# A gated block with dilated attention on one core: VectorE, ScalarE and POOL take program order, the softmaxes over head groups are weighted earlier, the pool mixer's gates come first

## Chip, cores and metric

One core of one Trainium2 chip. The metric is device time in microseconds. The change is compared with the kernel before it; a measurement of this kernel tells differences of about 0.3% from no change.

## What is computed

One decoder block on x (2048 tokens x 1024), in fp32, then a final RMSNorm. Cut to what matters:

```python
h = rmsnorm(x, norm_g) * (1 + scale) + shift             # scale, shift, gate = c @ w_ada + b_ada
qkv, z_attn, u_pool, z_pool, g_attn, g_pool = split(h @ w_in)
for gi, (win, dil) in enumerate(((128, 1), (512, 4), (2048, 16))):     # 8 heads of 64 each
    o, lse = dilated_window_attention(q, k, v, dil, win // dil, bias_g)
wts = softmax(stack(lses), axis=0)                        # over the three head groups
attn = sum(wts[..., None] * stack(outs), axis=0)
y_attn = (attn * silu(z_attn)) @ w_attn_br
pooled = multiscale_pool(u_pool)                          # trailing means over 2, 4, 8, 16 minus the token
mixed = einsum('bsgc,gce->bsge', pooled, pool_w) * pool_scale
y_pool = (mixed * silu(z_pool)) @ w_pool_br
merged = sigmoid(g_attn) * y_attn + sigmoid(g_pool) * y_pool
out = rmsnorm(x + gate * (merged @ w_out), final_g)
```

## The kernel before

The tokens are two halves `h` of 1024. Every big product is `mm3` (L247): operands are split into a high and a low fp32r part, and three products (hi hi, hi lo, lo hi) of two 128x512 matmuls each make a k-step, eight k-steps a 128x1024 tile in PSUM. Weights stream in through `fetch_raw` (a DMA on SyncE's queue) and `fetch_part`, which casts the high part on VectorE (L217) and subtracts the low part on POOL (L218).

For each half, four head pairs `hp` and three groups g in the order 1, 2, 0 make a `unit` (24 k-steps for the columns of k, q and v). `weave` runs the `attention` generator of the unit before inside it, some k-steps and then one step of attention. A step s of attention works on several pairs of 128-token tiles p at once: `transposed(s-2)` turns the exponentials (PE L717; VectorE L723, L726 and ScalarE L727 copy them to the single buffer pT), `output(s-3)` multiplies them with v (PE L738), `logits(s)` makes the next ones (PE L682, VectorE L686, ScalarE L692, VectorE L701, POOL L702), and `differences` (POOL L632) makes vd, with a single buffer, for the outputs. For g = 0 the outputs of the three groups are joined: `load_rows` fetches the other two groups' outputs and softmax terms, the weights are made by VectorE with one exp on ScalarE (L752 to L767), the three outputs are weighted and added (L770, L773), and in the next step `joined(s-4)` transposes the sum on PE (L777), after which ScalarE copies it to attnT (L779). PSUM tiles of `tp()` ("knot") have two buffers: output and joined of a step share one bank, transposed uses the other. Eight steps s = 0 to 7 make such an attention of g = 0; steps 3 to 7 are the ones in which output and joined run.

The last unit of a half (hp = 3, g = 0) is woven with `pool_in` instead of a unit: u's columns for the four groups of the pool mixer, a step each four k-steps. `pool_out` then makes the gates (zp's columns, sigmoid L820) and mixes. `branch`, `attn_gate`, `branch` and two `out_half` follow. In the second `out_half` of half 0, `next_h` prepares the normalised input of half 1: x tiles are loaded (`new_x`), squared and scaled (`x_norm`, ScalarE L293, POOL L282, VectorE L295) and transposed (`transposed_x`, PE L340, ScalarE L345).

After the first unit only PE and SyncE keep the order in which the program is written; the order on VectorE, ScalarE and POOL is chosen by a scheduler (L1051). The rotating buffers `b4` of the pool "big" are shared by nearly all of these tiles, so a load into one may wait for its last reader.

Of the kernel before, what the change touches and what calls it, by code (L numbers as in the profile page):

```python
# [11 lines left out]
F32 = mybir.dt.float32  # L12
# [56 lines left out]
def stream():  # L69
# [6 lines left out]
    seq += [("in", OFF_U + c * P, "col") for c in range(4)]  # L76
    seq += [("in", OFF_ZP + c * P, "col") for c in range(4)]
    for off, br in ((OFF_GP, "pbr"), (OFF_GA, "abr")):
# [68 lines left out]
def block_kernel(ctx: ExitStack, tc: tile.TileContext, x, cols, b_gate, w_ada, wpk, pool_w, rel_bias, final_g, onehot,  # L147
# [278 lines left out]
    def next_h(hp_, tiles):  # L426

        for p in range(0, 8, 2):
            for i, _ in enumerate(transposed_x(tiles[p:p + 2], p, hp_)):
                if p and p < 6 and i in (3, 4):  # L430
                    x_norm(tiles[p + i - 1])
                yield
            if p < 4:
                tiles += [new_x(1, p + 4), new_x(1, p + 5)]
# [150 lines left out]
    def attention(h, g, hp, res):  # L585
# [143 lines left out]
        def output(p, bank):  # L729
# [11 lines left out]
            if g:  # L741
# [16 lines left out]
            e = sm.tile([P, 2, 3, 2], F32, name="e")  # L758
# [26 lines left out]
        for s in range(7 if g else 8):  # L785
# [11 lines left out]
            for p in parts_:  # L797
                next(p, None)
# [12 lines left out]
            for p in parts_:  # L811
                next(p, None)
# [17 lines left out]
    def branch(hparts, gated, merged, mparts=None):  # L830
# [4 lines left out]
        for u in range(4):  # L835
# [3 lines left out]
            for j in range(2):  # L839
                ps = mm()  # L840
                yield from mm3(ps, take("col"), hparts)
# [7 lines left out]
                yield from mm3(ps, wb, gated, slice(j * P, (j + 1) * P), frees=(j == 1))  # L849
# [12 lines left out]
    def pool_in(h, hparts, pooled, todo):  # L862

        for gi in range(4):
            ps = mm()
            for _ in mm3(ps, take("col"), hparts):
                next(todo[0], None) if todo else None
                yield
            cur = b4(name="u0")
            nc.scalar.copy(out=cur, in_=ps)  # L870
            todo[:] = [chain(*todo, pool_sums(h, gi, cur, pooled))]

    def pool_sums(h, gi, u0, pooled):
# [25 lines left out]
        split(phi, plo, cur)  # L899
# [10 lines left out]

    def pool_out(hparts, pooled, gated, pwh, pwl, todo):
        for gi in range(4):
            ps = mm()
            for _ in mm3(ps, take("col"), hparts):
                next(todo[0], None)
                yield
            assert len(pooled) > gi
            sg = sigmoid(ps)
            nc.vector.tensor_tensor(out=sg, in0=ps, in1=sg, op=ALU.mult)
            phi, plo = pooled[gi]  # L920
            gsl = slice(gi * P, (gi + 1) * P)
            for q in range(2):
                sl = slice(q * 512, (q + 1) * 512)
                ps = bank(q)
                for i, (w, m) in enumerate(((pwh, phi), (pwh, plo), (pwl, phi))):
                    nc.tensor.matmul(ps, lhsT=w[:, gsl], rhs=m[:, sl], start=(i == 0), stop=(i == 2))  # L926
                nc.vector.scalar_tensor_tensor(out=sg[:, sl], in0=ps, scalar=psc_col[:, gi:gi + 1], in1=sg[:, sl],
                                               op0=ALU.mult, op1=ALU.mult)
            ghi, glo = b4(F32R, "gphi"), b4(F32R, "gplo")
            split(ghi, glo, sg)  # L930
# [205 lines left out]
```

## Time and profile before

| | us |
|---|---|
| median of 3 runs | 2218.45 |
| fastest, slowest run | 2213.07, 2219.28 |
| the profiled execution's own time | 2212.21 |
| its span, first to last instruction | 2210.2 |
| PE busy in it | 2137.7 (97%) |
| VectorE, ScalarE, POOL busy | 933.1, 597.6, 805.9 |
| mean granted TensorE clock | 0.989 |

All durations below come from that one profiled execution. [...] In the rows, the number in brackets behind an instruction is its engine's idle time before it, and what ended it.

### The profile page before, as it was taken

What the parts mean: (1) busy time and instruction counts of PE and PEld (TensorE: products, weight loads), DVE (VectorE), ACT (ScalarE), POOL (GpSimd) and SP (SyncE); (2) the same over time, 40 slices, a digit from 0 to 9 for tenths busy, and PEclk for the clock granted to TensorE, in tenths of its full rate; (3) what the DMA queues carried; (4) which work ended last, traced back from release to release, by engine and by line L of the source; (5) the groups of instructions that cost most, each with busy time, mean ns of one, the idle gap of its engine ahead of it and who ended that gap; (6) DMA issues with size and microseconds to landing.
All of it is one profiled execution on the core that took longest, in us unless ns stands there. A gap on an engine that the chain in (4) does not pass through costs nothing.

```text
span 2210.2 us, 30824 instructions
## 1 busy us (share of the span) xinstructions
PE 2137.7 (97%) x11786; PEld 1808.5 (82%) x11786; DVE 933.1 (42%) x2144; ACT 597.6 (27%) x1487; POOL 805.9 (36%) x669
## 2 busy tenths in 40 slices
PE   6999999999999999999799999999999999999998
PEld 4888888888878888889778878888888788888898
DVE  6536335263382111117743464553644831111164
ACT  4423333233321001003433333333333310010023
POOL 3313222132243225437743232332333432253375
PEclk9999999999999999999999999999999999999999
DMA  8442232222211112114432333223222111121134
GB/s 294 142 153 73 81 95 73 73 74 80 76 60 42 48 48 87 52 43 172 162 120 87 89 90 89 72 82 111 81 81 86 53 48 48 48 86 48 48 134 162
DMA packets 142675, 198.48 MB, mean 90 GB/s; under 512 B 13542, under 2 KB 109983, under 8 KB 142528
## 3 DMA queue, kind: packets, MB, share of 16 engines
q1 hardware_dynamic: 142528, 196.51, 27.9%
q8 instruction: 93, 1.52, 0.3%
q14 instruction: 54, 0.44, 0.1%
HBM read 157.62 MB, written 35.16 MB: 87 GB/s over the span
## 4 chain that ended last, share of the span: by engine, by line
PE 42%; DVE 3%; DMA 2%; issue 2%; POOL 2%; ACT 1%; SPq 0%; POOLq 0%; DVEq 0%; ACTq 0%
PE mm L255 33%; PE mm L1003 3%; PE knot L738 3%; PE qk L682 2%; DMA row<-rows 1%; POOL wlo L218 1%; PE knot L717 1%; PE knot L646 1%; ACT l L692 1%; DMA wraw<-in_wpk_dram 1%; DVE wd L762 0%; DVE l L701 0%; DVE whi L217 0%; PE hp L926 0%; POOL y L982 0%
## 5 line engine op out<-in xcount | busy, mean ns | idle before, releaser
L218 POOL TENSOR_TENSOR wlo<-wraw,whi 128x512 fp32r<-128x512 f32 x352 | 476.4, 1357 | 995.9 <-DVE whi L217 549.6
L255 PE MATMUL mm<-hhi,whi 128*128 128x512 f32 x2000 | 637.8, 400 | 0.0
L255 PE MATMUL mm<-hlo,whi 128*128 128x512 f32 x2000 | 621.4, 392 | 0.0
L255 PE MATMUL mm<-hhi,wlo 128*128 128x512 f32 x2000 | 619.5, 391 | 0.0
L217 DVE CAST whi<-wraw 128x512 fp32r<-128x512 f32 x349 | 189.6, 547 | 754.0 <-PE mm L255 628.7
L255 PEld LDWEIGHTS mm<-hhi,wlo 128*128 128x128 f32 x2000 | 377.4, 189 | 81.8
L255 PEld LDWEIGHTS mm<-hlo,whi 128*128 128x128 f32 x2000 | 377.1, 189 | 81.4
L255 PEld LDWEIGHTS mm<-hhi,whi 128*128 128x128 f32 x2000 | 364.7, 189 | 72.0 <-issue 0.5
L820 ACT ACTIVATE sg<-mm 128x1024 f32<-128x1024 f32 x48 | 49.4, 1028 | 555.1 <-PE mm L255 443.2
L686 DVE CUSTOM_DVE_ANT_0 l<-qk,bias 128x256 f32<-128x256 f32 (+1 forms) x384 | 126.0, 384 | 129.2 <-PE qk L682 105.9
L692 ACT ACTIVATE l<-l,row 128x256 f32<-128x256 f32 (+1 forms) x256 | 117.2, 460 | 149.0 <-DVE row L686 126.7
L1003 PE MATMUL mm<-whi,mhi 128*128 128x256 f32 x512 | 149.2, 291 | 1.0 <-DVE yt L1032 0.7
L1003 PE MATMUL mm<-whi,mlo 128*128 128x256 f32 x512 | 146.2, 286 | 2.5 <-POOL mlo L827 2.5
L1003 PE MATMUL mm<-wlo,mhi 128*128 128x256 f32 x512 | 145.9, 285 | 0.0
L738 PE MATMUL knot<-v,pT 128*128 128x64 f32 x768 | 131.5, 270 | 3.2 <-ACT pT L727 2.9
L738 PEld LDWEIGHTS knot<-v,pT 128*128 128x128 f32 x768 | 112.7, 193 | 5.7 <-ACT pT L727 3.2
L702 POOL TENSOR_TENSOR l<-l,ident 128x512 f32<-128x512 f32 (+1 forms) x56 | 71.6, 1278 | 108.5 <-DVE l L701 97.7
L738 PE MATMUL knot<-vd,pT 128*128 128x64 f32 x560 | 109.6, 278 | 1.3 <-DVE wd L762 1.3
L1003 PEld LDWEIGHTS mm<-whi,mlo 128*128 128x128 f32 x512 | 99.2, 194 | 3.3 <-POOL mlo L827 3.3
L1003 PEld LDWEIGHTS mm<-whi,mhi 128*128 128x128 f32 x512 | 99.5, 194 | 1.9 <-DVE yt L1032 1.5
L1003 PEld LDWEIGHTS mm<-wlo,mhi 128*128 128x128 f32 x512 | 99.5, 194 | 0.1
L727 ACT COPY pT<-knot 128x512 f32<-128x512 f32 x96 | 56.4, 588 | 155.1 <-PE knot L738 67.7
(175 smaller groups left out, 2497.3 us busy)
## 6 DMA issues: line engine op xcount, KB each, us to landing
wraw<-in_wpk_dram SPq DMA_DIRECT2D x176, 512.0 KB, 3.7
rows<-row SPq DMA_DIRECT2D x128, 66.0 KB, 1.7
row<-rows SPq DMA_DIRECT2D x64, 132.0 KB, 3.4
wada<-in_w_ada_dram SPq DMA_DIRECT2D x32, 256.0 KB, 5.5
x<-in_x_dram SPq DMA_DIRECT2D x16, 512.0 KB, 6.3
y<-in_x_dram SPq DMA_DIRECT2D x16, 512.0 KB, 7.7
out_dram<-yo SPq DMA_DIRECT2D x16, 512.0 KB, 6.5
khist<-kh SPq DMA_DIRECT2D x52, 128.0 KB, 2.5
```

The source lines that it names most:

```text
L217: copy(out=hi, in_=raw)
L218: nc.gpsimd.tensor_tensor(out=lo, in0=raw, in1=hi.bitcast(F32), op=ALU.subtract)
L255: nc.tensor.matmul(ps[:, n * 512:(n + 1) * 512], lhsT=w, rhs=m[:, n * 512:(n + 1) * 512], start=(k == 0 and j == 0), stop=(k == nk - 1 and ...
L646: nc.tensor.transpose(ps[:, (t % 4) * P:(t % 4) * P + P], res["vT"][:, k0:k0 + P], ident)
L682: nc.tensor.matmul(qks[i][:, j * 256:j * 256 + nk], lhsT=qt[qi][a], rhs=keys[ki][a], start=(n == 0), stop=(n == 2))
L686: nc.vector.tensor_tensor_reduce(out=l[:, 2 * j + i, 256 - nk:], in0=qks[i][:, j * 256:j * 256 + nk], in1=bt[:, i, 256 - nk:], scale=-1.0, ...
L692: nc.scalar.activation(out=ll, in_=ll, func=AF.Exp, scale=-1.0, bias=nd[:, j, i:i + 1], accum_out=nd[:, j, 2 + i:3 + i])
L702: nc.gpsimd.tensor_tensor(out=prev, in0=prev, in1=ident.unsqueeze(1).broadcast_to([P, 4 - f, P]), op=ALU.mult)
L727: nc.scalar.copy(out=pT[:, 1], in_=pps)
L738: nc.tensor.matmul(ops[:, j, hs], lhsT=d["pT"][:, b, 2 * j + i, :], rhs=vv[:, hs], start=(b == 1), stop=(b == 0 or not full))
L820: nc.scalar.activation(out=s, in_=ps, func=AF.Sigmoid)
L1003: nc.tensor.matmul(pst[:, pos:pos + 256], lhsT=st, rhs=mv, start=(fresh and i == 0), stop=(last and i == 2))
```

## The change

1. The manual schedule covers VectorE, ScalarE and POOL too, so that all five engines run in the order in which the program is written.
2. For g = 0 a new function `weights(p)` makes the weights of pair p, and weights and adds the two loaded groups, in step p + 3, between the VectorE work of `transposed` and that of `output`. The group's own output is added by four `scalar_tensor_tensor` (VectorE) that read PSUM, in place of ScalarE's copy (L751) and of the third plane of L770 and L773.
3. The pool mixer's gates (`pool_gates`: zp's columns, sigmoid) now come first, woven with the last attention of the half; u's columns follow (`pool_mix`, groups 3 down to 0), and each group's sums, mixing and split run as a generator `pool_group` that later k-steps `advance`, the last of them into the first product of `branch`.
4. `next_h` loads two x tiles at i = 3 instead of after i = 7 and runs `x_norm` at i = 4, 5 instead of 3, 4. In the output stage y is normalised in place, and yt, the gate's row and final_g's row move to buffers of the attention that are idle then, so that no x load waits for those.

```diff
+            r3, e = d["row3"], d["e"]
+            for j in range(2):
+                for i in range(2):
+                    hs = slice(i * 64, (i + 1) * 64)
+                    nc.vector.scalar_tensor_tensor(out=r3[:, j, 0, hs], in0=ops[:, j, hs], scalar=e[:, j, 2, i:i + 1],
+                                                   in1=r3[:, j, 0, hs], op0=ALU.mult, op1=ALU.add)
-            r3 = d["row3"]
-            nc.scalar.copy(out=r3[:, :, 2, 0:P], in_=ops)
-            nc.vector.tensor_copy(out=r3[:, :, 2, P:], in_=d["nd"])
-            yield
+        def weights(p):
+            d = st[p]
+            r3, nd = d["row3"], d["nd"]
+            nc.vector.tensor_copy(out=r3[:, :, 2, P:], in_=nd)
...
             for j in range(2):
-                ov = r3[:, j, :, 0:P].rearrange("p g (h c) -> p g h c", c=64)
-                nc.vector.tensor_tensor(out=ov, in0=ov, in1=e[:, j].unsqueeze(3).broadcast_to([P, 3, 2, 64]),
+                ov = r3[:, j, 0:2, 0:P].rearrange("p g (h c) -> p g h c", c=64)
+                nc.vector.tensor_tensor(out=ov, in0=ov, in1=e[:, j, 0:2].unsqueeze(3).broadcast_to([P, 2, 2, 64]),
                                         op=ALU.mult)
-            for i in (1, 2):
-                nc.vector.tensor_tensor(out=r3[:, :, 0, 0:P], in0=r3[:, :, 0, 0:P], in1=r3[:, :, i, 0:P], op=ALU.add)
+            nc.vector.tensor_tensor(out=r3[:, :, 0, 0:P], in0=r3[:, :, 0, 0:P], in1=r3[:, :, 1, 0:P], op=ALU.add)
...
-            for p in parts_:
+            for i, p in enumerate(parts_):
+                if i == len(parts_) - 1 - (s > 3) and g == 0 and 3 <= s < 7:
+                    weights(s - 3)
                 next(p, None)
...
-            for p in parts_:
-                next(p, None)
             yield
...
-                if p and p < 6 and i in (3, 4):
-                    x_norm(tiles[p + i - 1])
+                if p and p < 6 and i in (4, 5):
+                    x_norm(tiles[p + i - 2])
+                if p < 4 and i == 3:
+                    tiles += [new_x(1, p + 4), new_x(1, p + 5)]
...
-                    ctx.enter_context(tc.manual_schedule(engines={et.PE, et.SP}))
+                    ctx.enter_context(tc.manual_schedule(engines={et.PE, et.SP, et.DVE, et.Activation, et.Pool}))
...
-        weave(pool_in(h, hparts, pooled, todo), 32, queue, n_queue, 1)
-        run(queue)
-        run(pool_out(hparts, pooled, gated, pwh, pwl, todo))
-        run(branch(hparts, gated, merged))
+        weave(pool_gates(hparts, sgs), 32, queue, n_queue, 1)
+        run(queue)
+        todo = []
+        run(pool_mix(h, hparts, sgs, gated, pwh, pwl, todo))
+        run(branch(hparts, gated, merged, todo=todo))
```

How the order moves, at three places. The first is VectorE in the attention of g = 0, half 1, head pair 0, from step 3 to step 4; `row_...` is a pair's row3, numbered anew in each kernel. Before:

```order
L686 ISA nd 128x1
L773 TENSOR_TENSOR row_10665<-row_10665 128x2x128 x2
L701 TENSOR_TENSOR l<-l 128x4x128
L217 CAST whi<-wraw 128x512
L723 TENSOR_TENSOR pT<-knot,prevm 128x512
L770 TENSOR_TENSOR row_10738<-row_10738,e 128x3x128
L726 TENSOR_TENSOR pT<-pT,l 128x512
L770 TENSOR_TENSOR row_10738<-row_10738,e 128x3x128
L752 COPY row_10899<-nd 128x2x4
L563 SCALAR_TENSOR_TENSOR qlo_10844<-mm,qhi_10843 128x1024
```

And the same stretch after the change, from the end of step 3's transposed to step 4's:

```order
L726 TENSOR_TENSOR pT<-pT,l 128x512
L760 COPY row_10699<-nd 128x2x4
L763 TENSOR_REDUCE mn<-row_10699 128x4
L766 TENSOR_TENSOR e<-mn,row_10699 128x12
L769 TENSOR_TENSOR wd<-e,row_10699 128x12
L771 TENSOR_REDUCE sd<-wd 128x4
L773 RECIPROCAL sd<-sd 128x4
L774 TENSOR_TENSOR e<-e,sd 128x12
L777 TENSOR_TENSOR row_10699<-row_10699,e 128x2x128 x2
L779 TENSOR_TENSOR row_10699<-row_10699 128x2x128
L753 SCALAR_TENSOR_TENSOR row_10699<-knot,e,row_10699 128x64 x4
L686 ISA l,nd<-qk,bias 128x256
```

The whole weighting of a pair and the four reads of PSUM (L753) now stand in one piece between transposed's products and the next logits (L686), where before pieces of several pairs were mixed.

The second place is ScalarE in the same attention, steps 4 and 5 after the change (L767 is the weights' exp, L785 the copy of joined to attnT, L562 the high part of q of the unit that runs beside it):

```order
L692 ACTIVATE l,nd<-l,nd 128x256 x4
L727 COPY pT<-knot 128x512
L767 ACTIVATE e<-e 128x12
L785 COPY attnT_10532<-knot 128x256
L562 ACTIVATE qhi_10881<-mm 128x1024
L727 COPY pT<-knot 128x512
```

The copy to attnT stands ahead of q's high part, and no copy of the group's own output is left.

The third place is ScalarE in `next_h`, around the squares of the second pair of x tiles (L293) and those of the output stage (L983 before, L1008 in the change); L345 is the copy of a transposed tile. Before:

```order
L293 ACTIVATE junk,ssq<-x_8845 128x1024
L345 ACTIVATE hraw<-hp,shift_c,gmul 128x256
L983 ACTIVATE yt_9000,ssq_8598<-y_8596 128x256
L983 ACTIVATE yt_9000,ssq_8601<-y_8599 128x256
L983 ACTIVATE yt_9000,ssq_8604<-y_8602 128x256
L983 ACTIVATE yt_9000,ssq_8607<-y_8605 128x256
L293 ACTIVATE junk,ssq<-x_8847 128x1024
L345 ACTIVATE hraw<-hp,shift_c,gmul 128x256
```

After the change:

```order
L293 ACTIVATE junk,ssq<-x_8762 128x1024
L345 ACTIVATE hraw<-hp,shift_c,gmul 128x256
L293 ACTIVATE junk,ssq<-x_8764 128x1024
L345 ACTIVATE hraw<-knot,shift_c,gmul 128x256
L1008 ACTIVATE yt,ssq_8632<-y_8630 128x256
L1008 ACTIVATE yt,ssq_8635<-y_8633 128x256
```

The second tile's square now stands ahead of the output stage's four squares, not behind them.

## Rows read from the trace of the kernel before

**Rows 1.** The page's busy us, share of span, instructions, by engine

```profile
PE 2137.7 (97%) x11786; PEld 1808.5 (82%) x11786; DVE 933.1 (42%) x2144; ACT 597.6 (27%) x1487; POOL 805.9 (36%) x669
```

**Rows 2.** Stretches: length, busy us by engine, PEclk, DMA share, GB/s

```profile
200.00:240.00 40.00, 38.18 (x213) 31.69 (x212) 18.52 (x53) 11.70 (x37) 10.03 (x10) 0.96 0.31 94
600.00:640.00 40.00, 37.69 (x206) 31.56 (x204) 36.88 (x86) 12.22 (x36) 18.05 (x13) 0.91 0.15 50
640.00:680.00 40.00, 37.84 (x172) 31.12 (x172) 23.96 (x38) 9.49 (x12) 21.74 (x11) 1.00 0.18 53
1080.00:1120.00 40.00, 23.37 (x169) 22.78 (x168) 23.69 (x45) 16.70 (x42) 20.81 (x29) 0.79 0.27 93
1280.00:1320.00 40.00, 36.32 (x204) 30.36 (x203) 22.51 (x54) 12.27 (x32) 10.48 (x9) 0.96 0.27 76
1720.00:1760.00 40.00, 35.03 (x172) 29.60 (x171) 38.44 (x73) 10.51 (x25) 15.50 (x10) 0.91 0.22 63
...
1093.06:1097.06 4.00, 4.00 (x21) 4.00 (x22) 3.89 (x7) 1.02 (x2) 3.19 (x3) 0.56 0.02 6
```

**Rows 3.** PE's waits: us in total, times, longest us

```profile
PE knot L777 <- DVE row L773: 17.9, 11, 3.6
PE hp L340 <- DVE x L295: 16.6, 3, 8.0
...
PE knot L738 <- ACT pT L727: 2.9, 1, 2.9
...
PE hp L340 <- ACT hraw L345: 1.7, 1, 1.7
PE knot L738 <- DVE wd L762: 1.3, 1, 1.3
```

**Rows 4.** PE's timeline, one g = 0 unit: start us, us, instruction

```profile
1423.66 0.39 PE L738 MATMUL knot<-vd,pT 128*128 128x64 f32 x2
...
1429.54 0.33 PE L738 MATMUL knot<-v,pT 128*128 128x64 f32 x2
...
1436.09 0.33 PE L738 MATMUL knot<-v,pT 128*128 128x64 f32 x2
...
1439.84 0.44 PE L777 MATMUL knot<-ident,row 128*128 128x128 f32 x2 [1.85 <-DVE row L773]
...
1444.23 0.33 PE L738 MATMUL knot<-v,pT 128*128 128x64 f32 x2
...
1448.94 0.38 PE L777 MATMUL knot<-ident,row 128*128 128x128 f32 x2
```

**Rows 5.** VectorE's timeline in the same unit

```profile
1428.01 0.42 DVE L686 CUSTOM_DVE_ANT_0 l<-qk,bias 128x256 f32<-128x256 f32 x1
...
1430.65 0.70 DVE L701 TENSOR_TENSOR l<-l 128x512 f32<-128x512 f32 x1 [0.38 <-ACT l L692]
...
1433.17 1.78 DVE L726 TENSOR_TENSOR pT<-pT,l 128x512 f32<-128x512 f32 x1
...
1439.28 0.17 DVE L756 TENSOR_REDUCE mn<-row 128x4 f32<-128x12 f32 x1 [1.79 <-DMA row<-rows]
1439.37 0.41 DVE L773 TENSOR_TENSOR row<-row 128x256 f32<-128x256 f32 x1
...
1440.76 0.17 DVE L767 TENSOR_TENSOR e<-e,sd 128x12 f32<-128x12 f32 x1
```

**Rows 6.** POOL's timeline in the same unit

```profile
1432.79 1.60 POOL L218 TENSOR_TENSOR wlo<-wraw,whi 128x512 fp32r<-128x512 f32 x1
...
1438.13 0.72 POOL L632 TENSOR_TENSOR vd<-v 128x256 f32<-128x256 f32 x1 [2.59 <-DMA wraw<-in_wpk_dram]
```

**Rows 7.** Groups by line: busy us, mean ns, idle before

```profile
L727 ACT COPY pT<-knot 128x512 f32<-128x512 f32 x96 | 56.4, 588 | 155.1 <-PE knot L738 67.7 <-DVE pT L723 66.9 <-DVE row L752 11.3
...
L820 ACT ACT_TABLE_LOAD x2 | 2.6, 1283 | 4.0 <-PE mm L255 4.0
...
L404 DVE SCALAR_TENSOR_TENSOR gmul<-scale_c,col 128x2 f32<-128x2 f32 x4 | 0.9, 222 | 0.1
```

More of the change, by code (lines that the diff above doesn't have):

```diff
@@ L75, in stream @@
             seq += [("in", b + 512, "col"), ("in", b, "col"), ("in", b + 1024, "col")]
-    seq += [("in", OFF_U + c * P, "col") for c in range(4)]
     seq += [("in", OFF_ZP + c * P, "col") for c in range(4)]
+    seq += [("in", OFF_U + c * P, "col") for c in range(3, -1, -1)]
     for off, br in ((OFF_GP, "pbr"), (OFF_GA, "abr")):
@@ L828, in msplit, with branch @@
         return [(hi[:, j * 512:(j + 1) * 512], lo[:, j * 512:(j + 1) * 512]) for j in range(2)]
[L830 removed]
+    def branch(hparts, gated, merged, mparts=None, todo=()):
         add = bool(merged)
@@ L840, in branch @@
                 ps = mm()
-                yield from mm3(ps, take("col"), hparts)
+                for _ in mm3(ps, take("col"), hparts):
+                    advance(todo)
+                    yield
+                run(*todo)
                 sg = sigmoid(ps)
@@ L848, in branch @@
                 ps = mm()
-                yield from mm3(ps, wb, gated, slice(j * P, (j + 1) * P), frees=(j == 1))
+                turn = -1 if todo and not (u or j) else 1
+                yield from mm3(ps, wb[::turn], gated[::turn], slice(j * P, (j + 1) * P), frees=(j == 1))
                 msl = slice(j * 512, j * 512 + 512)
@@ L860, in branch, with pool_gates, pool_mix @@
             mparts += msplit(merged[0][3])
-    def pool_in(h, hparts, pooled, todo):
+    def pool_gates(hparts, sgs):
         for gi in range(4):
             ps = mm()
+            yield from mm3(ps, take("col"), hparts)
+            sg = sigmoid(ps)
+            nc.vector.tensor_tensor(out=sg, in0=ps, in1=sg, op=ALU.mult)
+            sgs.append(sg)
+    def pool_mix(h, hparts, sgs, gated, pwh, pwl, todo):
+        gated += [None] * 4
+        for gi in range(3, -1, -1):
+            ps = mm()
             for _ in mm3(ps, take("col"), hparts):
-                next(todo[0], None) if todo else None
+                advance(todo)
                 yield
@@ L870, in pool_in, with advance, pool_group @@
             nc.scalar.copy(out=cur, in_=ps)
-            todo[:] = [chain(*todo, pool_sums(h, gi, cur, pooled))]
+            todo.append(pool_group(h, gi, cur, sgs, gated, pwh, pwl))
+    def advance(gens):
+        for i in gens:
+            next(i, None)
+    def pool_group(h, gi, u0, sgs, gated, pwh, pwl):
+        pooled, n = [], 0
+        for _ in pool_sums(h, gi, u0, pooled):
+            n += 1
+            yield
+        for _ in range((7, 8, 10, 11)[gi] - n):
+            yield
+        sg = sgs[gi]
+        phi, plo = pooled[0]
+        gsl = slice(gi * P, (gi + 1) * P)
+        for q in range(2):
+            sl = slice(q * 512, (q + 1) * 512)
+            ps = bank(q)
+            for i, (w, m) in enumerate(((pwh, phi), (pwh, plo), (pwl, phi))):
+                nc.tensor.matmul(ps, lhsT=w[:, gsl], rhs=m[:, sl], start=(i == 0), stop=(i == 2))
+            nc.vector.scalar_tensor_tensor(out=sg[:, sl], in0=ps, scalar=psc_col[:, gi:gi + 1], in1=sg[:, sl],
+                                           op0=ALU.mult, op1=ALU.mult)
+        ghi, glo = b4(F32R, "gphi"), b4(F32R, "gplo")
+        split(ghi, glo, sg, nc.gpsimd if gi else nc.vector)
+        gated[gi] = ghi, glo
     def pool_sums(h, gi, u0, pooled):
@@ L909, in pool_weights @@
         return pwh, pwl
[L911 to L930, printed above, removed]
-            gated.append((ghi, glo))
     def attn_gate(h, hparts, gated):
@@ L989, in normed @@
             r = rstd(ssq, nc.gpsimd)
-            yo = b4(name="yo")
-            nc.vector.tensor_tensor(out=yo, in0=y, in1=fg_bc, op=ALU.mult)
-            nc.scalar.activation(out=yo, in_=yo, func=AF.Copy, scale=r)
+            for i in range(2):
+                sl = slice(i * 512, (i + 1) * 512)
+                nc.vector.tensor_tensor(out=y[:, sl], in0=y[:, sl], in1=fg_bc[i], op=ALU.mult)
+            nc.scalar.activation(out=y, in_=y, func=AF.Copy, scale=r)
             t0 = h * HALF + (4 * q + p) * P
-            store(out[t0:t0 + P, :], yo, 2)
+            store(out[t0:t0 + P, :], y, 2)
         for n in range(4):
@@ L1070, in block_kernel @@
         run(branch(hparts, gated, merged, m0))
-        rows_bc = b4(name="gate"), b4(name="fg")
+        rows_bc = (att.tile([P, D], F32, name="gate", tag="pT", bufs=1),
+                   [att.tile([P, 512], F32, name="fg", tag="bias", bufs=2) for _ in range(2)])
         nc.sync.dma_start(out=rows_bc[0], in_=gate_d)
-        nc.sync.dma_start(out=rows_bc[1], in_=final_g.partition_broadcast(P))
+        for i in range(2):
+            nc.sync.dma_start(out=rows_bc[1][i], in_=final_g[i * 512:(i + 1) * 512].partition_broadcast(P))
         mparts = []
```

10 lines of the change are left out of this document (4 added, 6 removed).

## The prediction

> **What bounds the kernel now.** I read the page's busy times first: PE is busy for 97% of the span [rows 1], so a change can only give back what PE spends idle or at its lower clock, and can only cost by making PE wait. Next, PE's waits by line [rows 3]: the joined transposes L777 wait 17.9 us for VectorE's last addition L773, 11 times; the transposes of half 1's input L340 wait 16.6 + 1.7 us; the last units add 2.9 and 1.3 us at L738. The start of the program waits too, and is not touched. Then the stretches [rows 2], for the clock: where PE had stood still for some us, its granted clock falls to the lower level. [...]
>
> Three places therefore have something to win. **The last unit of each half**: PE misses 2.31 + 2.16 us in the two stretches of half 0 and 4.97 us in that of half 1, 9.44 us in all; 0.91 over 40 us is 7.2 us at half rate, 3.6 us lost, twice: 16.6 us. **Six regular units of g = 0**: L777's 17.9 us less the last units' share of it (9.44 less L738's 4.2, so 5.2) leaves 12.7 us; three of the six show the 0.96 (the first and the last of these stretches are in the rows), 4.8 us: 17.4 us. **The input of half 1**: 18.3 us of waits. The clock is at 0.56 in the four us behind the longest of them, in which PE never stops; that is 3.5 us at half rate, 1.75 lost, and I count the same once more behind the last one (0.79 over 40 us has 16.8 us at the lower level, of which most lies in the waits themselves): 21.8 us.
>
> **Regular units of g = 0.** PE's order is the same; VectorE's is new. I follow one unit by PE's own times [rows 4] and VectorE's durations [rows 5].
>
> The price of one pair's weights: from L756's start to L767's end 1.65 us, the exp on ScalarE in it; with the copy ahead 1.75. Then three 256-element operations at 0.41 (two products, one addition), some 1.2 us: 2.95 us in a row. The four scalar_tensor_tensor of 64 elements don't occur before; below they are bounded by the same operation on two elements, 0.22 us [rows 7], whose start mostly overlaps, above by an L773 of four times the size, 0.41. I take 0.18 each, nearest to the first: 0.7 us. So 3.65 us, all in VectorE's order, and all ahead of the next logits.
>
> Step 3: PE ends output(0) at 1424.05; only then is the single pT free. L723 and L726 take 0.7 each, POOL's vd (0.72 [rows 6]) delays what follows by about 0.5: 1426.0. With 3.65 the weighting ends at 1429.7. PE's output(1), due at 1429.54, takes the same PSUM bank: it waits **0.25 us**.
>
> Step 4: the last logits stand behind that. From the first L686 to L701 pass 2.64 us, so L701 starts at 1432.3, L723 ends at 1433.5. POOL's L702 starts with L701's end, and an L726 beside a POOL operation takes 1.78 us instead of 0.7 [rows 5, 6]: 1434.9; vd again holds VectorE's next operations for some 0.65: 1435.55. With 3.65: 1439.2. ScalarE's copy to attnT (0.38) and a handover of 0.1: 1439.7. Output(2) is due at 1436.09 + 0.25 and takes the bank that all these read: it waits **3.35 us**.
>
> That the copy to attnT stands in this chain rests on one bank being read by two engines. In the trace ScalarE's L727 loses 66.9 us behind VectorE's L723 [rows 7], although both only read the same transposed bank. [...]
>
> Step 5: output(2) ends at 1441.45. q's high part, now behind the copy on ScalarE, and its low part on VectorE hold VectorE to 1441.85, a weight cast to 1442.25; L723 to 1442.85; L726 beside the cast's POOL operation L218 (1.3 to 1.6 us) to 1444.2, vd to 1444.9; 3.65 more: 1448.55. Joined(2) of step 6 was due at 1444.23 + 1.73 - 1.85 + 0.25 + 3.35 = 1447.7: **0.9 us**. Step 6: the next cast and its L218 (to 1450.2), then 3.65: 1453.9; joined(3) was due at 1448.94 - 1.85 + 4.5 = 1451.6: **2.3 us**.
>
> That is 6.8 us a unit. A wait of 3.35 us drops the clock as the one of 3.6 did, for 1.6 us; 0.9 of it falls where joined(2) would have waited anyway: 0.7. So 7.5 us a unit, 45.0 in six, against 17.4: **+27.6 us**. Whether POOL's operations meet VectorE's chain is the open part. If VectorE always goes first, step 4's vd and L702 (2 us) and step 6's L218 (1.3) drop out, and a unit loses some 3.8; if each meets it fully, three times another 1.1 us (1.78 less 0.69), 10.8.
>
> **Last units.** The same chain, but a step each four k-steps instead of three, as the program weaves them. Outputs are 6.55 us apart [rows 4]; some 2.5 of it are attention's own matmuls (output 1.73, the rest transposes), so a k-step is about 1.35 us, and three steps gain 4.0 us of the 7.5 and leave 3.5. The sigmoids of the gates stand between the exps, and each change of function loads a table: 12 more loads at 1.28 us [rows 7], 15.4 us of ScalarE, nearly all in its idle time; about half a load per half delays an exp, 0.6. So 4.1 in each half, 8.2 against 16.6: **-8.4 us**; nothing lost at all would be -16.6, the same waits as before no gain. The later groups' sums run under k-steps that PE has to do anyway; the last one (group 0) is needed at the end of branch's first product, where I see no more than a us of slack.
>
> [...]
>
> **Input of half 1.** The two x loads of a pair start four k-steps earlier and find free buffers; the second tile's square no longer stands behind the output stage's four squares. I take the longest wait, 8.0, as gone, the other 8.6 us of L340 as halved (4.3), the 1.7 as halved (0.8), the clock's 3.5 as 2.3, since a wait of 2 us can still drop it: 7.4 us against 21.8, **-14.4 us**. The ends are 0 and -21.8; of the three waits of x the longest is the one that the swapped rows explain whole.
>
> **The rest.** At the very end the reductions and products of the last two tiles alternate: +0.4. Units of g = 1 and 2 have no weights; program order can delay their loads of keys: +1.0 (0 to 5). The arithmetic that left (the third plane of L770, one L773, ScalarE's copy) ran beside PE: 0 in itself.
>
> **Sum**: 27.6 - 8.4 - 14.4 + 0.4 + 1.0 = **+6.2 us**. The profiled execution took 2212.2, 6.2 less than the median of the runs; on it the change gives 2218.4, on the median 2224.7.
>
> **The rivals.** (a) *POOL mostly loses the port*: a unit loses 3.8, 22.8 in six, +5.4 instead of +27.6, total -16.0: 2202.5. For it: VectorE is busy for only 42% of the span [rows 1], so most chains may find POOL idle; against: program order puts L726 right behind the L701 that starts POOL's L702. (b) *The weights are in time*, which is what moving them ahead would do if logits and pT did not hold them: each unit loses 1 us at most, -11.4 there, total -32.8: 2185.7. It decides if the weighting of pair 1 ends before PE wants output(2), at 1436.1; by the rows it ends three us later. (c) *Slower: POOL takes the port in the middle of each chain.* Three operations more stretched as L726 was, 3.2 us a unit, 19.2 in six: 2243.9. It decides if POOL's L218 and vd begin before the chain's first operation in steps 4, 5 and 6; the 1.78 us row speaks for it, the short operations of the chain, which can slip between, against. (d) *The reordering does not do what it says*: the scheduler before already kept these waits down as far as the data allow, the units stay at 17.4, and input and last units are held by other things: no change, 2218.5 to 2220.
>
> **How the numbers follow.** Forecast 0.45, with a range of its own from 2215 (units of 6) to 2236; (a) 0.22; (b) 0.10; (c) 0.17; (d) 0.06. A measurement tells 0.3%, 6.7 us: faster is below 2211.8, slower above 2225.1. Faster: (b) and most of (a), 0.27. Within: the lower half of the forecast, the rest of (a), and (d), 0.33. Slower: the forecast's upper half and (c), 0.40. The range 2194 to 2242 leaves out (b) and half of (c).
>
> **What would show it.** Right: in the six units PE waits at L738 for ScalarE's copy to attnT about 3 us at step 5 and at joined for L753 1 to 2 us at step 7, 40 us in all; L340 waits below 8 us; the windows of the last units at PE 38 or more of 40. Wrong: no L738 wait for the copy (then (b)); a wait of 5 us or more there, with L726 or the products above 1.5 us (then (c)); L340's longest wait still near 8 us.

## The result, and the profile after

The changed kernel takes 2248.18 us (median of 4 runs, 2247.62 to 2249.28), the kernel before 2217.9 beside it: a ratio of 1.0141, 95% interval 1.0123 to 1.0159. It is slower by 1.4%, some 30 us, where +6.2 was forecast and the range ended at 2242. The profiled executions have spans of 2245.8 and 2210.2 us; the account below is of these 35.6 us. The mean granted clock fell from 0.989 to 0.981.

The two programs give PE the same number of instructions, in the same order outside the pool stage, so the start of the n-th can be compared in the two traces. What the later one loses between two such marks is the difference of a stage (plus is time lost):

```
stage                                          forecast   after
start of the program                              0        -0.3
six regular units of g = 0                      +27.6     +24.5   (3.9 3.6 5.2 in half 0, 1.5 5.2 5.2 in half 1)
two last units, pool stage behind them           -8.4      -6.5
first output product of half 0, of half 1         0       +12.5, +6.3
input of half 1 (second output product)         -14.4      -1.6
units of g = 1 and 2                              +1.0       0.0
very end                                          +0.4      +0.7
```

**The units.** PE's waits by line in the changed kernel, the view of [rows 3]:

```profile
PE knot L738 <- ACT attnT L785: 22.8, 8, 3.2
PE hp L340 <- DVE x L295: 6.9, 3, 3.7
PE mm L1029 <- POOL wlo L218: 6.7, 6, 1.9
...
PE hp L340 <- ACT hraw L345: 3.6, 1, 3.6
PE mm L1029 <- DVE yt L1043: 3.6, 3, 1.7
...
PE knot L738 <- DVE row L753: 2.8, 6, 0.6
```

Joined, which waited 17.9 us before [rows 3], waits 2.3 us in all now; output waits for the copy to attnT instead, 3.15 to 3.17 us in each regular unit and 1.9 us in each of the last two. The timeline of VectorE in the unit of [rows 4, 5], 21.46 us later now:

```profile
1450.46 0.86 DVE L753 SCALAR_TENSOR_TENSOR row<-knot,e,row 128x64 f32<-128x64 f32 x4
...
1453.86 0.69 DVE L701 TENSOR_TENSOR l<-l 128x512 f32<-128x512 f32 x1 [1.17 <-ACT l L692]
1454.47 0.68 DVE L723 TENSOR_TENSOR pT<-knot,prevm 128x512 f32<-128x512 f32 x1
1455.26 1.22 DVE L726 TENSOR_TENSOR pT<-pT,l 128x512 f32<-128x512 f32 x1
...
1459.94 0.86 DVE L753 SCALAR_TENSOR_TENSOR row<-knot,e,row 128x64 f32<-128x64 f32 x4
```

ScalarE's in the same unit:

```profile
1460.89 0.37 ACT L785 COPY attnT<-knot 128x256 f32<-128x256 f32 x1 [3.13 <-DVE row L753]
1461.16 1.03 ACT L562 ACTIVATE qhi<-mm 128x1024 fp32r<-128x1024 f32 x1
```

And PE's:

```profile
1451.37 0.43 PE L738 MATMUL knot<-v,pT 128*128 128x64 f32 x2 [0.37 <-DVE row L753]
...
1461.31 0.43 PE L738 MATMUL knot<-v,pT 128*128 128x64 f32 x2 [3.17 <-ACT attnT L785]
```

The reads of the bank end at 1460.80; the prediction had 1439.2, with the 21.46 that is 1460.66. Output(2) waits 3.17 us (forecast 3.35). At steps 6 and 7 PE does not wait in this unit: from 1462.03 to 1468.85 its clock is 0.50, pairs of L255's matmuls start 0.85 us apart there and 0.47 behind it, and it asks later. Only two levels show in the two traces: in slices of half a us the kernel before (20 to 2200 us) has 83 at 0.50, 4262 at 1.00 and 15 between, the changed one (20 to 2240 us) 153, 4261 and 26; each of those between stands where one level passes into the other. So 0.91 over 40 us is 7.2 us at 0.50, and 0.96 is 3.2. The stretch 1440 to 1480 has 0.91, where the kernel before, with a wait of 1.85 us there [rows 4], had 1.00:

```profile
1440.00:1480.00 40.00, 36.46 (x195) 30.98 (x195) 27.09 (x86) 10.11 (x29) 11.74 (x11) 0.91 0.28 82
...
1036.00:1076.00 40.00, 30.78 (x216) 28.82 (x216) 18.11 (x30) 15.48 (x41) 23.44 (x25) 0.87 0.27 93
```

The unit of [rows 4] in the kernel before:

```profile
1420.00:1460.00 40.00, 38.15 (x228) 32.50 (x227) 26.20 (x71) 11.96 (x38) 12.37 (x10) 1.00 0.28 83
```

The second line of the changed kernel is the stretch in which half 0's first output product loses.

Three more of the six units look like this one. In the third unit of each half the stretch has 0.96, half as much at 0.50, and joined waits 0.8 us at step 7; no releaser is named, and VectorE's last L753 starts at 1623.16:

```profile
1600.00:1640.00 40.00, 35.64 (x196) 29.40 (x197) 23.74 (x79) 11.41 (x35) 10.02 (x8) 0.96 0.25 76
...
1623.74 0.67 PE L783 MATMUL knot<-ident,row 128*128 128x128 f32 x2 [0.82 <-issue]
```

They lose as much, 5.2 us: part of what the clock does not take there comes as a wait at joined.

**The output product.** There PE misses 9.22 of 40 us: 4.4 for weights whose low part is late, 1.5 for the high part, the rest for the product with the gate (yt). Its cause lies 30 us earlier, on POOL, at the end of the second branch:

```profile
999.32 1.29 POOL L218 TENSOR_TENSOR wlo<-wraw,whi 128x512 fp32r<-128x512 f32 x1 [9.64 <-DVE whi L217]
1006.60 7.77 POOL L833 TENSOR_TENSOR mlo<-mg,mhi 128x1024 fp32r<-128x1024 f32 x3 [5.98 <-ACT mhi L832]
1014.31 3.19 POOL L218 TENSOR_TENSOR wlo<-wraw,whi 128x512 fp32r<-128x512 f32 x2
```

The same engine and place in the kernel before, 9 us earlier by the clock of the trace:

```profile
990.41 1.30 POOL L218 TENSOR_TENSOR wlo<-wraw,whi 128x512 fp32r<-128x512 f32 x1 [9.64 <-DVE whi L217]
995.79 1.29 POOL L218 TENSOR_TENSOR wlo<-wraw,whi 128x512 fp32r<-128x512 f32 x1 [4.08 <-DVE whi L217]
997.68 2.40 POOL L827 TENSOR_TENSOR mlo<-mg,mhi 128x1024 fp32r<-128x1024 f32 x1 [0.60 <-ACT mhi L826]
1000.51 1.29 POOL L218 TENSOR_TENSOR wlo<-wraw,whi 128x512 fp32r<-128x512 f32 x1 [0.42 <-issue]
```

The scheduler put weights' low parts (L218) before and between the splits of merged. In program order all three splits come first, POOL stands idle for 5.98 us until ScalarE gives it the first, and the next L218 starts 15.0 us after the last (before: 5.4). On SyncE's queue the next raw weight waits for that L218 (26.0 us; 15.9 before), and the loads of gate, final_g and y wait behind it. SyncE's queue after the change:

```profile
973.42 43.00 SPq L203 DMA_DIRECT2D wraw<-in_wpk_dram  x4
1016.47 0.43 SPq L1099 DMA_DIRECT2D gate<-gate_d  x1
```

Before:

```profile
964.47 32.96 SPq L203 DMA_DIRECT2D wraw<-in_wpk_dram  x4
997.49 0.42 SPq L1072 DMA_DIRECT2D gate<-gate_d  x1
```

The weights come 10 us late, and VectorE stands for one, after the change:

```profile
1032.00 0.43 DVE L217 CAST whi<-wraw 128x512 fp32r<-128x512 f32 x1 [10.30 <-DMA wraw<-in_wpk_dram]
```

**The input of half 1.** The longest wait of L340 did go, 8.0 to 3.7 us [rows 3], and its 18.3 us fell to 11.0. With 1.4 us of another line (L1029) PE's waits in the stage are 12.4 us now, 5.9 less than before; yet the stage is only 1.6 us shorter. PE's own work in it takes 4.2 us longer (54.0 to 58.2), as more of it runs at the lower clock: PE is busy at 0.50 for 15.7 us of the stage, 7.2 before, added up over slices of 0.25 us; the clock's 0.88 and 0.86 below are means that count the waits too. The stage before:

```profile
1053.01:1125.29 72.28, 54.00 (x426) 53.11 (x425) 48.36 (x85) 31.18 (x72) 46.14 (x57) 0.88 0.41 146
```

After the change:

```profile
1074.44:1145.09 70.65, 58.21 (x426) 56.89 (x425) 47.08 (x89) 30.90 (x73) 43.20 (x54) 0.86 0.43 149
```

POOL and then VectorE show what the waits left are for:

```profile
1108.55 1.26 POOL L218 TENSOR_TENSOR wlo<-wraw,whi 128x512 fp32r<-128x512 f32 x1 [1.20 <-DVE whi L217]
1109.77 0.72 POOL L348 TENSOR_TENSOR hlo<-hraw,hhi 128x256 fp32r<-128x256 f32 x1
1110.57 0.19 POOL L280 TENSOR_SCALAR ms<-ssq 128x1 f32<-128x1 f32 x1
1110.85 0.55 POOL L282 TENSOR_TENSOR r<-ms,mhalf 128x1 f32<-128x1 f32 x1
```

```profile
1111.43 0.75 DVE L295 TENSOR_SCALAR x<-x,r 128x1024 f32<-128x1024 f32 x1 [2.77 <-POOL r L282]
```

The square of that tile ends at about 1108.1; its root stands in POOL's order behind a weight's and hlo's low part, and VectorE stands for it.

### The profile page after: what moved, and what is told of

Same layout as the page of the kernel before. It is cut to its first block, busy times and chain, and to the rows that moved or that the text cites. A ratio compares the mean times of both kernels' runs of the same rounds, so it can differ in the third digit from the quotient of the medians.

```text
span 2245.8 us, 30865 instructions
## 1 busy us (share of the span) xinstructions
PE 2161.8 (96%) x11786; PEld 1825.6 (81%) x11786; DVE 927.9 (41%) x2260; ACT 597.6 (27%) x1467; POOL 798.5 (36%) x665
## 4 chain that ended last, share of the span: by engine, by line
PE 41%; DVE 4%; POOL 3%; issue 2%; DMA 1%; ACT 1%; POOLq 0%; DVEq 0%; SPq 0%; ACTq 0%
PE mm L255 33%; PE knot L738 4%; PE qk L682 2%; POOL wlo L218 1%; DMA wraw<-in_wpk_dram 1%; PE knot L717 1%; PE mm L1029 1%; POOL y L1007 1%; PE knot L646 1%; DVE whi L217 0%; ACT l L692 0%; DVE y L1017 0%; DVE hhi L347 0%; POOL mlo L833 0%; DVE row L753 0%
## 5 line engine op out<-in xcount | busy, mean ns | idle before, releaser
L218 POOL TENSOR_TENSOR wlo<-wraw,whi 128x512 fp32r<-128x512 f32 x352 | 469.4, 1338 | 935.5 <-DVE whi L217 531.6
L255 PE MATMUL mm<-hhi,whi 128*128 128x512 f32 x2000 | 639.9, 401 | 0.0
L255 PE MATMUL mm<-hlo,whi 128*128 128x512 f32 x2000 | 622.6, 393 | 0.0
L255 PE MATMUL mm<-hhi,wlo 128*128 128x512 f32 x2000 | 619.4, 391 | 0.0
L255 PEld LDWEIGHTS mm<-hlo,whi 128*128 128x128 f32 x2000 | 378.3, 189 | 81.9
L255 PEld LDWEIGHTS mm<-hhi,wlo 128*128 128x128 f32 x2000 | 377.8, 189 | 82.0
L255 PEld LDWEIGHTS mm<-hhi,whi 128*128 128x128 f32 x2000 | 365.8, 190 | 72.1 <-issue 0.5
L686 DVE CUSTOM_DVE_ANT_0 l<-qk,bias 128x256 f32<-128x256 f32 (+1 forms) x384 | 126.0, 384 | 189.8 <-PE qk L682 173.2
L702 POOL TENSOR_TENSOR l<-l,ident 128x512 f32<-128x512 f32 (+1 forms) x56 | 71.4, 1275 | 267.9 <-DVE l L701 262.7
L1029 PE MATMUL mm<-whi,mhi 128*128 128x256 f32 x512 | 153.7, 300 | 7.2 <-DVE yt L1043 3.6
L738 PE MATMUL knot<-v,pT 128*128 128x64 f32 x768 | 135.6, 276 | 26.0 <-ACT attnT L785 22.8
L1029 PE MATMUL mm<-wlo,mhi 128*128 128x256 f32 x512 | 150.8, 295 | 6.7 <-POOL wlo L218 6.7
L1029 PE MATMUL mm<-whi,mlo 128*128 128x256 f32 x512 | 150.0, 293 | 2.1 <-POOL mlo L833 2.1
L727 ACT COPY pT<-knot 128x512 f32<-128x512 f32 x96 | 56.4, 588 | 317.8 <-DVE pT L723 241.8
L1029 PEld LDWEIGHTS mm<-whi,mhi 128*128 128x128 f32 x512 | 103.6, 202 | 9.1 <-DVE yt L1043 4.4
L1029 PEld LDWEIGHTS mm<-wlo,mhi 128*128 128x128 f32 x512 | 103.6, 202 | 8.2 <-POOL wlo L218 8.1
L1029 PEld LDWEIGHTS mm<-whi,mlo 128*128 128x128 f32 x512 | 103.5, 202 | 2.5 <-POOL mlo L833 2.5
```

What stands on the lines that cost most here:

```text
L218: nc.gpsimd.tensor_tensor(out=lo, in0=raw, in1=hi.bitcast(F32), op=ALU.subtract)
L255: nc.tensor.matmul(ps[:, n * 512:(n + 1) * 512], lhsT=w, rhs=m[:, n * 512:(n + 1) * 512], start=(k == 0 and j == 0), stop=(k == nk - 1 and ...
L686: nc.vector.tensor_tensor_reduce(out=l[:, 2 * j + i, 256 - nk:], in0=qks[i][:, j * 256:j * 256 + nk], in1=bt[:, i, 256 - nk:], scale=-1.0, ...
L702: nc.gpsimd.tensor_tensor(out=prev, in0=prev, in1=ident.unsqueeze(1).broadcast_to([P, 4 - f, P]), op=ALU.mult)
L727: nc.scalar.copy(out=pT[:, 1], in_=pps)
L738: nc.tensor.matmul(ops[:, j, hs], lhsT=d["pT"][:, b, 2 * j + i, :], rhs=vv[:, hs], start=(b == 1), stop=(b == 0 or not full))
```

## The experiments

Fifteen kernels. Ratios are to the kernel before, measured on the same chip beside each.

**e1: the scheduler back on three engines.**

```diff
-ctx.enter_context(tc.manual_schedule(engines={et.PE, et.SP, et.DVE, et.Activation, et.Pool}))
+ctx.enter_context(tc.manual_schedule(engines={et.PE, et.SP}))
```

> The changed kernel with VectorE, ScalarE and POOL given back to the scheduler (one line undone). If program order makes both losses, the output stage's 18.8 us go and the regular units fall well below their 6.9 us each: about 2205. If the units' loss lies in the code (four reads of the knot bank that the copy to attnT has to follow) whatever the order, only the output stage comes back: about 2228. If order is innocent: 2248.

2207.04 us, 0.9976 (0.9961 to 0.9990). All the rest of the change, without program order, takes about the time of the kernel before: 0.24% less, under the 0.3% that a measurement tells. The six units lose 1.6 us to it, not 24.5; the first output products lose 5.2 and 1.8, the input of half 1 gains 6.5, and the last units gain 17.1, of which the pool stage behind them gives 5.2 away. Program order makes nearly all of the units' loss and two thirds of the output products'. What keeps half 0's product 5 us late without it (3.9 in e3 below) was not looked for.

**e2: program order alone, on the kernel before.** The diff is e1's, the other way, in the kernel before.

> The kernel before with program order on all five engines and nothing else. If program order on POOL (three splits of merged ahead of the weights' low parts) makes the output stage's loss, PE shows it here too: some 12 us behind half 0's first output product and 6 behind half 1's. The joined softmaxes then stand behind the logits of their step, so L777 should wait 2 to 4 us in several steps of a unit. Together 2240 to 2260. If the output stage's loss comes from the moved buffers (yt, gate, final_g) instead, the output stage stays as in the kernel before and the time is below 2240.

2266.9 us, 1.0251 (1.0228 to 1.0274). Order alone costs more than the whole change: the six units +18.7, the last units +10.6, the output products +10.6 and +6.3 with buffers as before, the input of half 1 +4.9. L777's waits grow from 17.9 to 41.6 us:

```profile
PE knot L777 <- DVE row L773: 41.6, 18, 6.3
```

So the rest of the change does gain in program order, in the last units (+10.6 to -6.5) and in the input of half 1 (+4.9 to -1.6). The regular units are not among its gains: with the new weights they lose 24.5 us where program order alone loses 18.7, and 1.6 us under the scheduler (e1).

**e3: the splits spread.**

```diff
-                elif u == 3 and add:
-                    for i in range(3):
-                        mparts += msplit(merged[0][i])
...
-                yield from mm3(ps, wb[::turn], gated[::turn], slice(j * P, (j + 1) * P), frees=(j == 1))
+                for k, _ in enumerate(mm3(ps, wb[::turn], gated[::turn], slice(j * P, (j + 1) * P), frees=(j == 1))):
+                    if add and u == 3 and j and k in (0, 1, 2):
+                        mparts += msplit(merged[0][k])
+                    yield
```

> The changed kernel with the three splits of merged at the end of the second branch made one per k-step of the product that follows, not all ahead of it, so that a weight's low part can run on POOL between them. If the late weights come from that block, most of the 18.8 us of the output stage go: 2230 to 2234. If they come from the x and y loads that share the queue, or from the buffers that moved, under 5 us go: 2243 or more.

2232.72 us, 1.0096 (1.0072 to 1.0121): 15.5 us back from the change's 2248.18. The output products stand at +3.9 and -1.2. POOL now:

```profile
1005.80 1.30 POOL L218 TENSOR_TENSOR wlo<-wraw,whi 128x512 fp32r<-128x512 f32 x1 [4.13 <-DVE whi L217]
1007.65 4.96 POOL L833 TENSOR_TENSOR mlo<-mg,mhi 128x1024 fp32r<-128x1024 f32 x2 [0.56 <-ACT mhi L832]
1012.58 1.75 POOL L218 TENSOR_TENSOR wlo<-wraw,whi 128x512 fp32r<-128x512 f32 x1
```

**e4: ScalarE copies the output out of PSUM first.**

```diff
-            r3, e = d["row3"], d["e"]
+            r3 = d["row3"]
+            nc.scalar.copy(out=r3[:, :, 2, 0:P], in_=ops)
+            yield
+            e = d["e"]
...
-                    nc.vector.scalar_tensor_tensor(out=r3[:, j, 0, hs], in0=ops[:, j, hs], ...
+                    nc.vector.scalar_tensor_tensor(out=r3[:, j, 0, hs], in0=r3[:, j, 2, hs], ...
```

The weights follow all the copies of the step.

> The changed kernel, but ScalarE again copies the group's own output out of PSUM, and the copy to attnT follows at once; the weights come after both, and the four scalar_tensor_tensor read SBUF. If the bank chain makes the units' loss, PE's wait at output for the copy to attnT (22.8 us, 8 times) is gone, joined waits 1 to 2 us in one or two steps, and six units give back 15 to 22 us: 2226 to 2234. If the weights' place ahead of the logits makes it, PE waits as long at pT or at joined instead: 2243 or more.

2230.15 us, 1.0088 (1.0065 to 1.0111): 18 us back, 11.0 in the six units (24.5 to 13.5) and 6.9 in the last ones. The wait for the copy is gone; joined waits for VectorE in its place:

```profile
PE knot L786 <- DVE row L756: 24.2, 19, 1.7
```

As many us in waits, but none over 1.75, and in this execution five of the six units show a clock of 1.00 (mean 0.991). Two of the other three have 0.984 and 0.986 and are 3 to 6 us longer.

**e5: weights ahead of transposed in the step.** The call of `weights(s - 3)` stands ahead of the loop over `parts_`.

> The changed kernel with the weights ahead of transposed's VectorE work in the same step, so that they run while PE does the k-steps between two steps. If the units lose because the weighting stands between pT and the four reads of the bank, PE's waits for the copy to attnT (22.9 us) go and six units give back most of their 24.5 us: 2222 to 2230. If VectorE is simply too full in such a unit, or the rows land too late for it, PE waits as before at another place: 2240 or more.

2247.35 us, 1.0144 (1.0129 to 1.016): nothing; the six units still lose 22.9 us. The other reading was right. VectorE takes 9.37 us from one L723 to the next, and stands in them only for ScalarE's exps (1.17 us) and the weights' own exp (0.28):

```profile
1301.93 0.69 DVE L723 TENSOR_TENSOR pT<-knot,prevm 128x512 f32<-128x512 f32 x1
...
1306.73 0.69 DVE L701 TENSOR_TENSOR l<-l 128x512 f32<-128x512 f32 x1 [1.17 <-ACT l L692]
...
1311.30 0.69 DVE L723 TENSOR_TENSOR pT<-knot,prevm 128x512 f32<-128x512 f32 x1
```

PE's step is 6.55 us. Whatever the order within it, the chain of a step that has both logits and weights is longer; the wait moved to the bank of transposed (PE's L717 for ScalarE's L727, 15.0 us in 8).

**e6: x_norm two k-steps earlier.** `if p and p < 6 and i in (2, 3): x_norm(tiles[p + i])`.

> The changed kernel with x_norm at i = 2, 3 in next_h (the kernel before had 3, 4, the change 4, 5). If the waits of L340 left after the change (6.9 us of x, with the clock behind them some 10) come from POOL taking the root of the squares' sum only behind the weights' and hlo's low parts of the same k-step, two k-steps more hide it: 8 to 11 us less, 2237 to 2240. If x itself lands too late, PE or ScalarE waits for the load: 2246 to 2252.

2248.06 us, 1.015 (1.0135 to 1.0165): nothing either. From the first L340 to the end of the stage PE's waits for x fall from 6.9 to 1.5, and others take their place:

```profile
PE knot L340 <- ACT hraw L345: 4.7, 2, 3.4
...
PE mm L1029 <- DVE yt L1043: 3.4, 1, 3.4
PE hp L340 <- DVE x L295: 1.5, 1, 1.5
```

It was not x landing late, as the other reading had it: neither theory named this. VectorE still stands 2.8 us for each second tile's root, and what is behind it in the order is late.

**e7, e8: the mends together, in program order and in the scheduler's.** e7 joins e3, e5 and e6; e8 is e1 with e3 and e6.

> The three mends together, all engines in program order: splits spread, weights first, x_norm earlier. If the three losses are apart from one another, they add up: 15.5 less for the splits, some 20 for the weights, some 9 for x_norm: 2200 to 2207, as fast as the scheduler's order or faster. If program order costs something of its own that none of the three touches, it stays above 2211.

> The scheduler's order for VectorE, ScalarE and POOL with the splits spread and x_norm earlier. If the scheduler already puts the weights' low parts between the splits and the root ahead of them, nothing moves: 2205 to 2209. If the same two places bind there as well (half 0's output product is 5 us late, L340 waits 10 us), 5 to 10 us go: 2197 to 2202.

e7: 2232.59 us, 1.0083 (1.0065 to 1.01), which is e3's 2232.72. e8: 2208.24 us, 0.9968 (0.9957 to 0.9979), which is e1's. So the expected 2200 to 2207 did not come: of the three mends only the splits gain in program order, and under the scheduler neither the splits nor x_norm gains.

**e9, e10, e11: one engine at a time given back.** In e1's line only `et.DVE`, `et.Pool` or `et.Activation` is left out.

> The changed kernel with VectorE alone given back to the scheduler; ScalarE and POOL keep program order. The theory now: a unit's loss is VectorE's chain of one step in program order (some 9.4 us from one L723 to the next where logits, weights and reads follow one another, with 1.2 us in it waiting for the exps) against PE's 6.6 us; the output stage's loss is POOL's order. Then the regular units give back most of their 24.5 us and the output stage keeps 10 or more: 2220 to 2230. If ScalarE's order (copy to attnT behind, q's high part) makes the units' loss, 2240 or more.

> The changed kernel with POOL alone given back to the scheduler. By the theory the output stage gives back 15 to 19 us (as with the splits spread) and the units nothing: 2229 to 2234. If the units' loss comes from POOL's operations that hold VectorE's port, they give back some of it too: below 2225.

> The changed kernel with ScalarE alone given back to the scheduler. By the theory neither place moves, and only the first wait in the input of half 1 (3.6 us, behind three scalings of y on ScalarE) can go: 2242 to 2249. If ScalarE's order is what makes the copy to attnT late, the units gain 10 us or more: below 2238.

e9 2240.73 us, 1.0121 (1.0104 to 1.0138); e10 2239.76, 1.0117 (1.0101 to 1.0134); e11 2245.69, 1.0143 (1.0126 to 1.016), the change's own.

With POOL free the output products stand at +3.8 and -0.8, and the units at +25.9: POOL's order makes the one loss and not the other. Its time is above the expectation, because the last units and the pool stage lose 7.5 us more than in the change. With VectorE free the units stand at +14.5, with ScalarE free at +24.5; the output products keep 9.3 and 6.3 with VectorE free. So VectorE's order alone explains 10 of the units' 24.5 us, less than expected. With VectorE free, PE's wait has moved: it is 2.0 us for the copy to attnT, and at output it waits for the reads of the bank themselves:

```profile
PE knot L738 <- DVE row L753: 19.0, 8, 3.3
```

Looked at in one unit (1440 to 1445 us), the scheduler has put the last logits and L701 ahead of pair 0's four reads, and VectorE works through without a wait. All three free (e1) leave 1.6 us; two engines free together were not tried, so how the other 13 us divide among the three orders is open.

**e12: e3 and e4 together, in program order.**

> All engines in program order, the splits spread and the group's own output copied by ScalarE (the two mends that gained alone, 15.5 and 18.0 us). If they are apart from one another they add up: 2213 to 2217, and the time of the kernel before is reached in program order.

2216.77 us, 1.0009 (0.9999 to 1.002). The two add up nearly (15.5 + 18.0 off 2248.2 would be 2214.7).

**e13: the scheduler's order, with e3 and e4.**

> The scheduler's order for VectorE, ScalarE and POOL with the splits spread and ScalarE's copy of the group's own output back. If the read of one bank by two engines costs something even where the scheduler chooses, 3 to 8 us go against 2207: 2199 to 2204. If the scheduler already keeps the bank free in time (PE waited 3.0 us in all for the copy to attnT there), the extra copy buys nothing: 2205 to 2212.

2193.61 us, 0.991 (0.9894 to 0.9926): the fastest of all, 0.9% below the kernel before. The six units now gain 8.7 us against it, where e1 lost 1.6. The splits, with x_norm, had gained nothing there (e8), so this is the copy, and it is worth more under the scheduler's order than expected. The rows suggest why, though no run separates the two: the bank is free after a ScalarE copy of 0.4 us (377 ns for one of that size, L743 in the changed kernel), and VectorE, whose order is free, fills part of its wait for the exps between L686 and L701 with pieces of the weights of two pairs:

```profile
1405.63 0.17 DVE L766 TENSOR_REDUCE mn<-row 128x4 f32<-128x12 f32 x1
...
1406.30 0.29 DVE L769 TENSOR_TENSOR e<-mn,row 128x12 f32<-128x12 f32 x2
...
1406.91 0.69 DVE L701 TENSOR_TENSOR l<-l 128x512 f32<-128x512 f32 x1
```

Output waits 6.8 us for ScalarE's part of pT in all, and neither joined nor the copy to attnT stands among PE's longer waits.

**e14, e15: the chain shortened at one place.** The addition L701 of the last logits, with POOL's L702, is made a step later, behind transposed's work; e14 in the change (its diff follows), e15 in e12, there behind all the copies of the step.

```diff
-            f = d["from"] = nks.count(P) * 2
-            if f == 4:
+            d["from"] = nks.count(P) * 2
+            if g or p < 3:
+                fold(p)
+
+        def fold(p):
...
+            late = g == 0 and s == 4
             for i, p in enumerate(parts_):
+                if i == 1 and late:
+                    fold(s - 1)
```

> The changed kernel with one thing moved: the addition of the last logits' two halves (L701, and POOL's L702 behind it) is made in step 4 behind transposed's work, not in step 3, where VectorE stands 1.2 us for ScalarE's exps. If the chain in program order on VectorE is what holds the bank, PE's wait at step 5 falls from 3.15 by about the 0.9 us that L702 leaves of it, and six units give back 5 to 9 us with the clock: 2238 to 2243. If the bank is held by something else, PE waits 3.1 us as before: 2246 to 2250.

> The same move on top of the two mends that added up (splits spread, copy back; 2216.8). Joined still waits there 18.6 us for the four reads at the chain's end; by the chain theory each of the six units gains 1 to 1.5 us: 2208 to 2212. Otherwise 2215 to 2218.

e14: 2244.48 us, 1.0135 (1.0119 to 1.0151). The wait at step 5 falls from 3.17 to 2.76 us, in all six units from 24.5 to 22.3:

```profile
PE knot L744 <- ACT attnT L791: 19.5, 8, 2.8
```

The direction is the chain theory's, the size under half of it. L702 now runs beside the weights, and in the changed kernel an L766 beside POOL's L218 takes 1.11 us (1470.80) where the median is 0.17; that this makes the rest of the difference was not shown. e15: 2208.78 us, 0.9971 (0.996 to 0.9982), 8 us below e12, as expected: in program order on all engines the kernel then takes 0.3% less than before, the least that a measurement tells.

## Why the prediction was wrong

**The units of g = 0: right in mechanism, place and size** (+27.6, measured +24.5). In the unit that it followed every step of the chain up to output(2) came out within 0.2 us: the price of a pair's weights, the last logits behind them, L701 after the exps, POOL's part of L726 and the vd, and ScalarE's copy behind the reads of the bank. The copy waits 3.13 us for VectorE (L785's row above) although both only read that bank; and e4, which takes VectorE's reads off the bank, gives 11 us back in these units. What the copy's place behind those reads costs by itself no run tests. Mis-sized were steps 6 and 7: of 0.9 and 2.3 us of joined waits none came in four units and 0.8 us in two. In the four, PE then ran at 0.50 for some 7 us (6.8 in this unit, 1462.03 to 1468.85), not 3.2 as assumed: 3.4 us lost, an estimate that takes half of it, instead of the 0.7 put down. The two errors cancel, and that the sum came within 3 us is in that part luck. The clock's terms in the sum (3.6 twice, 4.8, 3.5, 0.7) take PE at the lower level to do half its work; by the pairs' distances above, 0.85 us against 0.47, it loses 45% there.

**The last units: right** (-8.4, measured -6.5, of which -7.9 in the units and +1.4 behind them). ScalarE's table loads after the change, by line:

```profile
L826 ACT ACT_TABLE_LOAD x8 | 10.3, 1283 | 0.1
L767 ACT ACT_TABLE_LOAD x4 | 5.1, 1283 | 0.1
L692 ACT ACT_TABLE_LOAD x3 | 3.8, 1283 | 0.1
```

With the start's one they are 12 more than before, each 1283 ns again, and no wait of PE is put down to one.

**"The rest: program order can delay their loads of keys: +1.0"** is the step that failed. I looked for what program order does in the units, and gave everything else one us. The first output products, which the sum does not even name, lost 18.8 us, 16 of them from three splits on POOL, in a stage 30 us before the one that pays. The order of the changed kernel was there to be read, and POOL's rows of the kernel before show L218 between the splits; I asked only of the places where PE already waited. e3 and e10 settle it: either gives back 16 of the 18.8 us, and e2 shows the loss with the old buffers.

**The input of half 1, -14.4, was -1.6.** The swap of the squares did end the longest wait. Mis-sized were both parts of the term: the waits were to fall by 13.2 us (18.3 to 5.1) and fell by 5.9, and the clock was to give 1.2 us back and took 4.2 more. What I left out is that program order also binds POOL's roots and VectorE's scaling to the weights and hlo of the same k-step, and the first copies of the stage to three scalings of y on ScalarE (3.6 us, 1.7 before). By itself program order costs 4.9 us there (e2); under the scheduler the same edits gain 6.5 (e1). e6 showed that moving x_norm only hands the wait on. Which of the three engines' orders binds last there is left open; with ScalarE free the stage gains 5.6 in the profiled execution, but that one was 5 us shorter than the kernel's other three.

**The rivals.** (c) came within 5 us of the time by another cause: its extra waits inside the units did not appear, and POOL's free order (e10) leaves the units as they are. (a), (b) and (d) fell. What (a), (c) and e10's expectation call the port is a reading of the rows, and no run shows what the two engines share; measured is an L726 of 0.69 us with POOL idle (1441.92) and of 1.78 beside L218 and vd [rows 5, 6], and of 0.89 to 1.22 beside POOL in the followed unit after the change. The split of the chances was also wrong in kind: all cases but (d) took the gains elsewhere as given, and no case had program order cost something where PE did not wait before.

## What to carry to other kernels

An edit that fixes the order on a whole engine is priced at every place where the old order interleaved two streams, not only where PE waits now: compare the orders of the two programs for each engine through the whole program, and look for blocks of one kind that hold back a feeder of DMA queues. In a pipelined step compare an engine's whole chain in order, its waits for other engines included, with the step's length; where it was longer here, moving a piece within the step gained nothing (e5), and filling the waits (e14) or freeing the buffer earlier (e4) did. Where the read of a PSUM bank stands at the end of one engine's long queue, the bank was held here for all of it (22.8 us of PE's waits); a short copy by an idle engine can be worth more than the operation it saves (18 us in e4, some 14 in e13).

## What was not expected of the hardware

The length of PE's wait did not tell how far the clock fell. In the kernel before, three waits for joined can be compared. One of 3.63 us stands in a stretch at 0.96, 3.2 us at 0.50 (1280 to 1320 [rows 2]), and one of 1.85 us in a stretch at 1.00. But one of 1.82 us stands in a stretch at 0.96 too (200 to 240 [rows 2]):

```profile
205.93 0.69 PE L777 MATMUL knot<-ident,row 128*128 128x128 f32 x2 [1.82 <-DVE row L773]
```

In the changed kernel every regular unit has a wait of 0.4 to 0.6 us and, ten us later, one of 3.15 to 3.17 us; the stretch around it has 0.91 in four units and 0.96 in two. In e4's profiled execution many waits of at most 1.75 us, 24.2 us in all, leave five of six units at 1.00. So several short waits cost less clock there than a long one of the same sum, but what decides between 1.00, 0.96 and 0.91 was not tried.
